# Local attention of a gated block: the next queries are transposed first in a round, the late query embeddings are spread over the seam and rounds 0 to 9, and the first loads come in another order

## The chip, the cores and the metric

The kernel runs on one core of a Trainium2 chip. The metric is the device time of one execution in microseconds (us). The kernel before takes 1314.7 us, the median of three runs between 1314.09 and 1314.88 us. A core has five engines that run side by side, each through its own list of instructions: PE (matrix products; PEld is its loading of weights), DVE (elementwise work), ACT (copies, scaling, exponentials), POOL (more elementwise work) and SP, which here only issues transfers (DMAs).

## The reference, cut to what matters

One decoder block in float32 over 1024 tokens of width 1024. Only the first half concerns the change: a projection, rotary embedding ("rope") of queries and keys, and attention over a window of 128 tokens, cut into blocks of 128 queries that each see their own and the previous block of keys.

```python
def rmsnorm(x, g):
    xf = x.astype(jnp.float32)
    xf = xf * lax.rsqrt(jnp.mean(xf * xf, axis=-1, keepdims=True) + EPS)
    return (xf * g.astype(jnp.float32)).astype(x.dtype)

def apply_rope(x, cos, sin):
    x1, x2 = jnp.split(x.astype(jnp.float32), 2, axis=-1)
    return jnp.concatenate([x1 * cos - x2 * sin, x2 * cos + x1 * sin], axis=-1)

# in reference():
h = rmsnorm(x, mix_norm_g[l])
proj = h @ w_in[l]
qa, ka, va, q_lat, kv_lat, k_r, g_a, g_b = jnp.split(proj, IN_OFFSETS, axis=-1)
qa = apply_rope(qa.reshape(B, S, SWA_HEADS, HEAD_DIM), cos_a, sin_a)   # 8 heads of 64
ka = apply_rope(ka.reshape(B, S, SWA_KV_HEADS, HEAD_DIM), cos_a, sin_a)  # 2 groups
o_a = swa_sink_attention(qa, ka, va, swa_sinks[l])   # window 128, blocks of 128
...
o_b = mla_attention(q_nope, q_rope, k_nope, k_rope, vb)
y = jax.nn.sigmoid(g_a) * (o_a @ w_o_swa[l]) + jax.nn.sigmoid(g_b) * (o_b @ w_o_mla[l])
x = x + y @ w_out[l]
h = rmsnorm(x, ffn_norm_g[l])
x = x + (silu(h @ w_gate[l]) * (h @ w_up[l])) @ w_down[l]
return rmsnorm(x, final_norm_g)
```

## The kernel before

A float32 product is done as three products of rounded halves: both operands are split into a high part (a copy that rounds, on ACT) and a low part (the difference, on DVE), and PE adds high by high, high by low and low by high; lines L305 to L307 are these three. So nearly every operand of PE is made by ACT and then DVE.

The program has these stretches, by the time at which PE works on them:

- 0 to 42 us: the query latents, one tile `ql` for each of eight rows of 128 tokens. The rows come in the order 0, 4, 1, 5, 2, 6, 3, 7. Rows 0 and 4 start from the raw transposed input (`xt`) and the raw weights (`wr`, line L877, four loads), the later ones from the normalised input.
- 38 to 128 us: seven products `st` that stand for the four quarters of the rest of the projection (`product`), each over two halves of the depth and four row blocks `t`. Out of these come queries, keys, values and key latents. Those of blocks 0 to 3 are ready first. Blocks 4 to 7 are "late": their queries are sums of two products, built in the tiles called `w` here and stored to memory (`q_d`, L1287 and L1290).
- 122 to 130 us: the seam, where the last products and the first scores overlap.
- 130 to 300 us: sixteen rounds `it` of local attention (the loop at L1353), one for each pair of head group and block. `ITS` gives their order: group 0 blocks 0 to 3, group 1 blocks 0 to 3, group 0 blocks 4 to 7, group 1 blocks 4 to 7. Each round also holds three products of 12 matmuls (`gate_step`) of the gate projection, whose results are `fa` and `fb`.
- after 300 us: the latent attention, the output projections and the feed-forward part.

In a round the steps for three different blocks are interleaved. For the next block, it+1, `sw_qT` transposes the queries on PE (two matmuls `qT`, L755); ACT copies the high parts (L758, L759), DVE subtracts the low parts (L760, L761) and so makes the tile `qs`; `sw_scores` then does eight matmuls `sc` (L774) with `qs` and the keys `khd`. For the present block, `sw_pT` transposes the probabilities, and for the previous one `sw_pv` multiplies with the values (`o`, L829 and L830). The queries of block it+2 are loaded from `q_d` into `qn` by `sw_q` (L733); those of late blocks are rotated after that by `late_q`, four instructions on DVE (two at L469, one each at L471 and L472).

PE and SP follow the order in which the program is written. In the first 130 us the program itself is ordered by a planner (`beg`, steps are added by `go`): each step has an engine, a cost, what it comes after and sometimes a due time `by`, and the planner lays out all five engines from them. SP's loads have fixed ranks there in the order in which `load_step` is called. In the rounds a scheduler places the instructions of ACT, DVE and POOL.

Of the kernel before, what the change touches and what calls it, by code (L numbers as in the profile page):

```python
# [8 lines left out]
F32 = mybir.dt.float32  # L9
# [8 lines left out]
P = 128  # L18
S = 1024
# [210 lines left out]
def hybrid_block_kernel(  # L230
# [633 lines left out]
    def load_step(*name, kb, emit, use=(), after=()):  # L864
        go("L", *name, eng="S", cost=2000 + kb * 2.6, emit=emit, after=after, use=use, rank=next(turn_of) - 1e6)

    def load_xt(b, k0, k1):
        if b not in xt:
            xt[b] = U("xt", F32, (P, NK, P))
        nc.sync.dma_start(xt[b][:, k0:k1], x_t[b][:, k0:k1])  # L870
# [36 lines left out]
    def ql_load(j):  # L907
        load_step("w", j, kb=416, emit=lambda: load_ql(j), use=(("U", ("wr", j)),))
# [7 lines left out]

    load_step("x", "0a", kb=256, emit=lambda: load_xt(0, 0, 4), use=(("U", ("xt", 0)),))
    ql_load(0)
    load_step("x", 0, kb=256, emit=lambda: load_xt(0, 4, NK), after=[("L", "w", 0)])
    ql_load(1)  # L920
    xt_load(4)
    ql_load(2)
    ql_load(3)
    for i, rows_ in enumerate(((1, 5), (2, 0, 6), (3, 4, 7))):
        for b_ in rows_:
            xs_load(b_)
            if b_ not in RAWS:
                xt_load(b_)
        if i == 1:
            load_step("t", 0, kb=512, emit=lambda: load_tables(0), use=(("U", "t0"),))  # L930
# [49 lines left out]
    for b in ROWS:  # L980
# [7 lines left out]
        go("nm", b, eng="D", cost=1300, emit=lambda b=b: normalize(b), after=[("sp", b), *raw_lo] + [("h0", 1)] * (b == 0), give=("rb", b))  # L988
        for kh in range(2):
            if b in RAWS and b:  # L990
                quad_steps(b, kh, ("rh", "rl"), [("L", "x", b)])
            if (b, kh) != (4, 0):
                quad_steps(b, kh, ("bh", "bl"), [("nm", b)] + [("ql", b)] * (b in RAWS))

# [223 lines left out]
    def kv_steps(b, src, after, by, port):  # L1218
# [2 lines left out]
        go("k3", b, eng="P", cost=600, after=[("km", b)], emit=lambda: rstd_in(rs_k[:, b:b + 1]))  # L1221
        go("k5", b, eng="S", cost=2500, after=[("k4", b)], by=by, emit=lambda: kv_store(b), free=(("kl", b),))

    for t in range(4):
        o = t % 2

# [57 lines left out]
           emit=lambda t=t, c_of=c_of: add(half_of("w2", t), c_of(5), half_of("w2", t), nc.vector))  # L1284
        kv_steps(t + 4, lambda t=t: half_of("w2", t)[:, 256:512], [("C22", t)], 128 + 2 * t, True)
        go("k4", t + 4, eng="D", cost=450, port=True, after=[("k3", t + 4)], emit=lambda t=t: kv_norm(half_of("w2", t)[:, 256:512], t + 4))
        go("qo", t + 4, eng="S", cost=2500, after=[("C22", t)], by=120 + t, emit=lambda t=t: nc.sync.dma_start(q_d[t + 4], half_of("w2", t)[:, 0:256]))  # L1287
        go("C12", t, eng="D", cost=690, after=[("M", 3, 1, t)], by=121 + 1.4 * t, give=("st", 5, t),
           emit=lambda t=t, c_of=c_of: add(half_of("w1", t), c_of(3), half_of("w1", t), nc.vector))
        go("qp", t + 4, eng="S", cost=2500, after=[("C12", t)], by=124 + t, emit=lambda t=t: nc.sync.dma_start(q_d[NB + t + 4], half_of("w1", t)[:, 0:256]))  # L1290
# [50 lines left out]
        k_high(b)  # L1341
        k_low(b)

    def late_q(it):
        b = ITS[it][1]
        qn = sw[it]["qn"]
        rope_nat(halves(qn[:, 0:256], 32), 4, 32, tl_["rope_a"][:, 0, b], tl_["rope_a"][:, 1, b], [halves(qn[:, 0:256], 32)])

    N_SW = 2 * NB
    gates.load_part(1, 0)  # L1350
    V_SUM = {0: (0, 0, 3), 3: (1, 0, 3), 6: (0, 3, 7), 9: (1, 3, 7)}
    V_PART = {2: (0, 0, 3), 5: (1, 0, 3), 8: (0, 3, 7), 12: (1, 3, 7)}
    for it in range(N_SW):  # L1353
        if it + 2 < N_SW:
            sw_q(it + 2)
        if it in V_PART:
            v_parts(*V_PART[it])
        gate_step()
        if it + 1 < N_SW:
            sw_qT(it + 1)  # L1360
        if it in (1, 2, 4, 5):
            late_row({1: 4, 2: 5, 4: 6, 5: 7}[it])
        gate_step()
        if it + 1 < N_SW:
            sw_scores(it + 1)
        if it in (2, 3, 5, 6):
            late_k({2: 4, 3: 5, 5: 6, 6: 7}[it])
        if it + 2 < N_SW and ITS[it + 2][1] > 3:
            late_q(it + 2)
        if it == N_SW - 1:  # L1370
            st.load_to(st.index[("uq", 0)])
            load_lat(4)
        if it >= 1:
            sw_pv(it - 1)
        if it in V_SUM:
            v_sums(*V_SUM[it])
        gate_step()
        sw_pT(it)
        if it + 1 < N_SW:
            sw_exp(it + 1)  # L1380
# [1211 lines left out]
```

## Time and profile before

| | |
|---|---|
| median of 3 runs | 1314.7 us (1314.09 to 1314.88) |
| the profiled execution's own time | 1313.86 us |
| its span, first to last instruction | 1312.1 us |
| PE busy | 1295.6 us, 99% of the span |
| DVE, ACT, POOL busy | 73%, 50%, 43% |
| TensorE's granted clock | 0.999 of full speed on average |

The profiled execution lies 0.84 us below the median. What a stretch costs is read from its own rows, since the share of busy time is a mean over stretches with different limits. In the rows, "idle before" is how long the engine waited, and the arrow names what released it. Matmuls overlap, so their time is read best from the start of one to the start of the next.

### The profile page before, as it was taken

To read this page: it belongs to the slowest core of one execution; us is meant where nothing else is said; L and a number is where in the kernel's file an instruction comes from. 1 tells how busy PE (TensorE), PEld (TensorE's weight loads), DVE (VectorE), ACT (ScalarE), POOL (GpSimd) and SP (SyncE) were. 2 spreads that over 40 slices of the span, in tenths; PEclk is the share of its full clock that TensorE was granted. 3 is DMA by queue.
4 is the path that set the end of the run, shared out by engine and by line. 5 is a ranking of instruction groups with operands and counts; after the bars stand their busy time and mean duration, and the time that the engine had idled before them with its cause. 6 is when DMAs were issued, how large, how long until landed. Compare 5 with 4: busy or idle time off the path is not lost.

```text
span 1312.1 us, 18158 instructions
## 1 busy us (share of the span) xinstructions
PE 1295.6 (99%) x6223; PEld 1082.1 (82%) x6223; DVE 952.2 (73%) x1548; ACT 649.9 (50%) x1299; POOL 561.0 (43%) x518
## 2 busy tenths in 40 slices
PE   9999999999999999999999999999999999999997
PEld 6878787888888888888888888888888888888886
DVE  6998778986778874688889765676666555663964
ACT  7853675675577786644465232232323323634341
POOL 3202557663423365310224468775567621022521
PEclk9999999999999999999999999999999999999999
DMA  9312322436500203895321345743454335995504
GB/s 365 141 47 81 117 101 73 133 105 212 165 17 9 73 34 113 310 267 161 121 89 49 128 154 207 288 171 136 158 184 169 135 126 201 386 383 196 177 16 145
DMA packets 79692, 201.54 MB, mean 154 GB/s; under 512 B 10160, under 2 KB 16816, under 8 KB 78896
## 3 DMA queue, kind: packets, MB, share of 16 engines
q1 hardware_dynamic: 76720, 193.57, 41.3%
q0 software_dynamic: 1440, 4.72, 1.9%
q10 hardware_dynamic: 1440, 2.10, 0.4%
q8 instruction: 49, 0.80, 0.2%
q14 instruction: 43, 0.35, 0.1%
HBM read 138.88 MB, written 57.28 MB: 149 GB/s over the span
## 4 chain that ended last, share of the span: by engine, by line
PE 87%; DVE 4%; ACT 4%; DMA 3%; issue 1%; SPq 0%; POOL 0%; DVEq 0%; ACTq 0%
PE fa L305 8%; PE fa L307 8%; PE fa L306 8%; PE fb L305 6%; PE fb L307 6%; PE fb L306 6%; PE fd L306 5%; PE fd L307 5%; PE fd L305 5%; PE pTb L1763 2%; PE xo L306 2%; PE xo L307 2%; PE xo L305 2%; DMA x<-in_x_dram 1%; PE st L305 1%; PE st L307 1%
## 5 line engine op out<-in xcount | busy, mean ns | idle before, releaser
L299 DVE TENSOR_TENSOR wl<-wr,wl 128x512 fp32r<-128x512 f32 x145 | 148.2, 1044 | 62.1 <-ACT wl L298 61.3
L299 DVE TENSOR_TENSOR lrv<-lr,lrv 128x1024 fp32r<-128x1024 f32 x77 | 105.0, 1396 | 48.4 <-ACT lrv L298 43.0
L298 ACT CAST lrv<-lr 128x1024 fp32r<-128x1024 f32 x77 | 80.1, 1052 | 94.4 <-PE fd L307 58.6
L305 PE MATMUL fd<-lrv 128*128 128x512 f32 x308 | 119.8, 389 | 0.0
L306 PE MATMUL fd<-lrv 128*128 128x512 f32 x308 | 119.8, 389 | 0.0
L307 PE MATMUL fd<-lrv 128*128 128x512 f32 x308 | 119.8, 389 | 0.0
L1747 POOL TENSOR_SCALAR p<-p,denb 128x384 f32<-128x384 f32 (+3 forms) x64 | 48.0, 753 | 89.5 <-DVE denb L1743 75.2
L298 ACT CAST wl<-wr 128x512 fp32r<-128x512 f32 x145 | 83.9, 620 | 1.9 <-PE fa L307 1.6
L299 DVE TENSOR_TENSOR wl<-sm,wl 128x512 fp32r<-128x512 f32 x58 | 52.0, 920 | 30.0 <-ACT wl L298 29.8
L313 POOL TENSOR_TENSOR wr<-wr,sm 128x512 f32<-128x512 f32 x20 | 30.5, 1529 | 95.1 <-DVE wl L299 95.1
L305 PEld LDWEIGHTS fd<-lrv 128*128 128x128 f32 x308 | 57.8, 188 | 12.1
L306 PEld LDWEIGHTS fd<-lrv 128*128 128x128 f32 x308 | 57.8, 188 | 12.0
L307 PEld LDWEIGHTS fd<-lrv 128*128 128x128 f32 x308 | 57.8, 188 | 11.8
L2226 ACT ACTIVATE act<-sm 128x512 f32<-128x512 f32 x11 | 7.0, 632 | 104.1 <-DVE sm L310 104.1
L310 DVE TENSOR_TENSOR ptl<-pTb,pth 128x512 fp32r<-128x512 f32 (+2 forms) x96 | 49.5, 548 | 9.2 <-ACT pth L1774 8.8
L313 POOL TENSOR_TENSOR sm<-wr,wr 128x512 f32<-128x512 f32 (+1 forms) x36 | 41.3, 1153 | 32.1 <-DMA wr<-in_w_gate_dram 28.4
L1733 DVE CUSTOM_DVE_ANT_0 scb<-scb,mask 128x384 f32<-128x384 f32 (+3 forms) x64 | 48.3, 760 | 7.9 <-PE scb L1720 7.4
L1738 ACT ACTIVATE p<-scb,nmb 128x384 f32<-128x384 f32 (+3 forms) x64 | 47.9, 748 | 11.8 <-DVE nmb L1733 8.0
L1774 ACT CAST pth<-pTb 128x512 fp32r<-128x512 f32 (+2 forms) x96 | 43.1, 484 | 10.8 <-PE pTb L1763 10.5
L2226 ACT ACTIVATE act<-pu 128x512 f32<-128x512 f32 x22 | 13.9, 633 | 67.5 <-DVE pu L310 36.7
L305 PE MATMUL fb<-t3h,wl 128*128 128x512 f32 x120 | 47.3, 395 | 0.0
L305 PE MATMUL fb<-t2h,wl 128*128 128x512 f32 x120 | 47.2, 393 | 0.0
(435 smaller groups left out, 4209.6 us busy)
## 6 DMA issues: line engine op xcount, KB each, us to landing
lr<-la_d SPq DMA_DIRECT2D x77, 256.0 KB, 5.4
wr<-in_w_gate_dram SPq DMA_DIRECT2D x22, 512.0 KB, 4.7
wr<-in_w_up_dram SPq DMA_DIRECT2D x22, 512.0 KB, 5.3
la_d<-sd SPq DMA_DIRECT2D x22, 512.0 KB, 4.8
wd<-in_w_down_dram SPq DMA_DIRECT2D x22, 512.0 KB, 7.0
rb_d<-wd SPq DMA_DIRECT2D x22, 512.0 KB, 2.7
lr<-rb_d SPq DMA_DIRECT2D x44, 256.0 KB, 5.4
lr<-in_w_down_dram SPq DMA_DIRECT2D x33, 256.0 KB, 5.4
```

Source lines behind the costliest of these rows:

```text
L298: nc.scalar.copy(hi, src)
L299: (eng or nc.vector).tensor_tensor(lo, src, hi.bitcast(F32), op=ALU.subtract)
L305: nc.tensor.matmul(ps, ah, bh, start=first and i == 0, stop=False, skip_group_check=go_on)
L306: nc.tensor.matmul(ps, ah, bl, start=False, stop=False, skip_group_check=go_on)
L307: nc.tensor.matmul(ps, al, bh, start=False, stop=last and i == n - 1, skip_group_check=go_on)
L310: eng.tensor_tensor(out, a, b, op=ALU.subtract)
L313: eng.tensor_tensor(out, a, b, op=ALU.add)
L1733: nc.vector.tensor_tensor_reduce(s_, s_, m_, 1.0, -NEG, op0=ALU.add, op1=ALU.min, accum_out=nm)
L1738: nc.scalar.activation(p_, s_, AF.Exp, scale=-1.0, bias=t_.pop(("nm", key)), accum_out=den)
L1747: nc.gpsimd.tensor_scalar(p[:, 0:w], p[:, 0:w], den, 0.0, op0=ALU.mult, op1=ALU.add)
L1763: nc.tensor.transpose(pp[:, k], t_["p", key][:, blk(4 * g + k)], ident)
L1774: nc.scalar.copy(hi, pp)
```

## The change

There are three parts.

1. First loads. The second weight tile is loaded before the second half of the first input tile. Input tile 4 (512 KB) is loaded in two halves of 256 KB, after all four weight tiles; its second half is planned behind the first.
2. Order of a round. `sw_qT(it + 1)` comes ahead of the round's first `gate_step`. Two products instead of one stand between the transposes and the scores.
3. Late queries. Group 0's late queries are rotated before they are stored: those of t = 0 and 1 as planned DVE steps in the seam (with stores that wait for them), those of t = 2 and 3 in rounds 0 and 3. Group 1's four late blocks are loaded together (512 KB, in round 5) and rotated in rounds 6 to 9. No round loads or rotates a single late query any more.

```diff
     load_step("x", "0a", kb=256, emit=lambda: load_xt(0, 0, 4), use=(("U", ("xt", 0)),))
     ql_load(0)
+    ql_load(1)
     load_step("x", 0, kb=256, emit=lambda: load_xt(0, 4, NK), after=[("L", "w", 0)])
-    ql_load(1)
-    xt_load(4)
     ql_load(2)
     ql_load(3)
+    load_step("x", "4a", kb=256, emit=lambda: load_xt(4, 0, 4), use=(("U", ("xt", 4)),))
+    load_step("x", 4, kb=256, emit=lambda: load_xt(4, 4, NK), after=[("L", "x", "4a")])
...
-                quad_steps(b, kh, ("rh", "rl"), [("L", "x", b)])
+                quad_steps(b, kh, ("rh", "rl"), [("L", "x", "4a" if kh == 0 else b)])
...
+    def late_q0(t):
+        w = half_of("w2", t)[:, 0:256]
+        rope_nat(halves(w, 32), 4, 32, tl_["rope_a"][:, 0, t + 4], tl_["rope_a"][:, 1, t + 4], [halves(w, 32)])
+
+    def q0_out(t):
+        nc.sync.dma_start(q_d[t + 4], half_of("w2", t)[:, 0:256])
...
-        go("qo", t + 4, eng="S", cost=2500, after=[("C22", t)], by=120 + t, emit=lambda t=t: nc.sync.dma_start(q_d[t + 4], half_of("w2", t)[:, 0:256]))
+        if t < 2:
+            go("rr", t, eng="D", cost=1380, port=True, after=[("C22", t)], by=133 + t, emit=lambda t=t: late_q0(t),
+               use=(("U", ("rr", t)),), free=(("rr", t),))
+            go("qo", t + 4, eng="S", cost=2500, after=[("rr", t)], emit=lambda t=t: q0_out(t))
...
-    def late_q(it):
-        b = ITS[it][1]
-        qn = sw[it]["qn"]
-        rope_nat(halves(qn[:, 0:256], 32), 4, 32, tl_["rope_a"][:, 0, b], tl_["rope_a"][:, 1, b], [halves(qn[:, 0:256], 32)])
+    q1 = []
+
+    def late_q1(t):
+        if not q1:
+            q1.append(U("q1", F32, (P, 4, 256)))
+            nc.sync.dma_start(q1[0], q_d[NB + 4:2 * NB].rearrange("b p c -> p b c"))
+        else:
+            w = q1[0][:, t]
+            rope_nat(halves(w, 32), 4, 32, tl_["rope_a"][:, 0, t + 4], tl_["rope_a"][:, 1, t + 4], [halves(w, 32)])
+            sw[12 + t] = {"qn": w}
...
     for it in range(N_SW):
-        if it + 2 < N_SW:
+        if it + 2 < 12:
             sw_q(it + 2)
         if it in V_PART:
             v_parts(*V_PART[it])
-        gate_step()
         if it + 1 < N_SW:
             sw_qT(it + 1)
+        gate_step()
         if it in (1, 2, 4, 5):
             late_row({1: 4, 2: 5, 4: 6, 5: 7}[it])
+        if it in (0, 3):
+            late_q0({0: 2, 3: 3}[it])
+            q0_out({0: 2, 3: 3}[it])
         gate_step()
         if it + 1 < N_SW:
             sw_scores(it + 1)
         if it in (2, 3, 5, 6):
             late_k({2: 4, 3: 5, 5: 6, 6: 7}[it])
-        if it + 2 < N_SW and ITS[it + 2][1] > 3:
-            late_q(it + 2)
+        if it == 5:
+            late_q1(0)
+        if 6 <= it < 10:
+            late_q1(it - 6)
```

The same numbers of matmuls, copies and rotations are done as before. Since the planner lays out the whole first stretch anew, its instructions also change places among themselves.

On PE, this is where the queries of a round are transposed; it is round 8, whose scores are those of block 9 in the order of `ITS` (`fb` and `fa` are gate products, `pT` the probabilities; a row of dots leaves out the rest of a product). Before, from the end of the round's first product to the scores:

```order
L307 MATMUL fb_2267<-t3h_712,wl_2262 128x512
L755 MATMUL qT_2379<-ident,qn_2229 128x128 x2
L305 MATMUL fa_2399<-t1h_984,wl_2316 128x512
...
L307 MATMUL fa_2399<-t1h_984,wl_2316 128x512
L774 MATMUL sc_2414<-khd_1217,qs_2382 128x256
```

And now, from the transposed probabilities of the round before:

```order
L815 MATMUL pT_2360<-ident,pe_2191 128x128 x4
L755 MATMUL qT_2381<-ident,qn_2252 128x128 x2
L305 MATMUL fb_2290<-t3h_693,wl_2285 128x512
...
L307 MATMUL fb_2290<-t3h_693,wl_2285 128x512
L305 MATMUL fa_2422<-t1h_986,wl_2339 128x512
...
L307 MATMUL fa_2422<-t1h_986,wl_2339 128x512
L774 MATMUL sc_2437<-khd_1219,qs_2384 128x256
```

The two transposes moved past one whole product; the scores stay where they were.

On DVE, this is the end of the seam, from the last of the first block's four maxima to the second block's low parts (`khd` are keys, `pu` a gate result, `lat` key latents, `w` with L469 a late query that is rotated). Before:

```order
L790 TENSOR_TENSOR es_1287<-nm_1285,nsink 128x4
L310 TENSOR_TENSOR khd_1217<-kT_1266,khd_1217 128x128
L310 TENSOR_TENSOR khd_1218<-kT_1266,khd_1218 128x128
L310 TENSOR_TENSOR khd_1217<-kT_1304,khd_1217 128x128
L310 TENSOR_TENSOR khd_1218<-kT_1304,khd_1218 128x128
L313 TENSOR_TENSOR w_117_866<-st_1120,w_117_866 128x512
L299 TENSOR_TENSOR vv_844<-w_117_866,vv_844 128x2x64
L313 TENSOR_TENSOR pu_1337<-fb_1354,pu_1337 128x512
L760 TENSOR_TENSOR qs_1342<-qT_1339,qs_1342 64x2x128
L761 TENSOR_TENSOR qs_1342<-qT_1339,qs_1342 64x2x128
```

And now:

```order
L790 TENSOR_TENSOR es_1308<-nm_1306,nsink 128x4
L310 TENSOR_TENSOR khd_1219<-kT_1286,khd_1219 128x128
L310 TENSOR_TENSOR khd_1220<-kT_1286,khd_1220 128x128
L1214 SCALAR_TENSOR_TENSOR lat_1235<-w_129_964,rs_k,tab_298 128x256
L469 TENSOR_TENSOR rp_1356<-w_129_964,tab_554 128x256
L760 TENSOR_TENSOR qs_1336<-qT_1333,qs_1336 64x2x128
L761 TENSOR_TENSOR qs_1336<-qT_1333,qs_1336 64x2x128
L469 TENSOR_TENSOR rp_1356<-w_129_964,tab_554 128x256
L299 TENSOR_TENSOR wl_1364<-wr_975,wl_1364 128x512
L471 TENSOR_TENSOR w_129_964<-rp_1356 128x4x32
L472 TENSOR_TENSOR w_129_964<-rp_1356 128x4x32
L313 TENSOR_TENSOR pu_1354<-fb_1369,pu_1354 128x512
```

The gate result and a pair of keys no longer stand ahead of the low parts; one key latent and half of a rotation do.

On SP, these are the first loads (`xt` 163 is input tile 0; `xt` 174 before and 192 now is tile 4). What was and what now stands, as a difference:

```order
 L877 DMA wr_167<-in_w_ql_dram 128x832
-L870 DMA xt_174<-in_x_t_dram 128x1024
+L877 DMA wr_174<-in_w_ql_dram 128x832
 L870 DMA xt_163<-in_x_t_dram 128x512
 L877 DMA wr_183<-in_w_ql_dram 128x832
-L877 DMA wr_192<-in_w_ql_dram 128x832
-L434 DMA x_198<-in_x_dram 128x1024
-L870 DMA xt_210<-in_x_t_dram 128x1024
+L870 DMA xt_192<-in_x_t_dram 128x512
+L434 DMA x_199<-in_x_dram 128x1024
+L870 DMA xt_205<-in_x_t_dram 128x1024
+L870 DMA xt_192<-in_x_t_dram 128x512
```

Input tile 4 moved from the fourth place to the seventh and the tenth; from the load behind that on the two lists agree.

## Rows read from the trace of the kernel before

**Rows 1.** The page: busy time, share of the span and instructions of each engine.

```profile
PE 1295.6 (99%) x6223; PEld 1082.1 (82%) x6223; DVE 952.2 (73%) x1548; ACT 649.9 (50%) x1299; POOL 561.0 (43%) x518
```

**Rows 2.** Waits of PE, 130 to 306 us: us in total, times, longest.

```profile
PE sc L774 <- DVE qs L760: 2.1, 3, 1.3
PE sc L774 <- DVE qs L761: 0.8, 5, 0.2
```

**Rows 3.** Timeline of PE, block 1: start, us, instruction, [idle before <-releaser].

```profile
131.18 0.38 PE L755 MATMUL qT<-ident,qn 128*128 128x128 f32 x2
...
133.95 0.39 PE L307 MATMUL fb<-t2h,wl 128*128 128x512 f32 x1
135.62 0.39 PE L774 MATMUL sc<-khd,qs 128*128 128x256 f32 x1 [1.29 <-DVE qs L760]
136.17 1.07 PE L774 MATMUL sc<-khd,qs 128*128 128x256 f32 x7 [0.16 <-DVE qs L761]
137.08 0.40 PE L305 MATMUL fa<-hh,wl 128*128 128x512 f32 x1
```

**Rows 4.** Timeline of PE, block 2.

```profile
143.05 0.38 PE L755 MATMUL qT<-ident,qn 128*128 128x128 f32 x2
...
145.79 0.39 PE L307 MATMUL fa<-t1h,wl 128*128 128x512 f32 x1
...
146.97 0.40 PE L829 MATMUL o<-pth,vv 128*128 128x512 f32 x1
```

**Rows 5.** Timeline of PE, blocks 6, 9 and 12, ahead of and behind the scores.

```profile
189.13 0.39 PE L307 MATMUL fa<-hh,wl 128*128 128x512 f32 x1
...
191.15 0.39 PE L496 MATMUL kT<-ident,kd 128*128 128x128 f32 x2
...
222.93 0.39 PE L307 MATMUL fa<-t1h,wl 128*128 128x512 f32 x1
...
225.37 0.40 PE L829 MATMUL o<-pth,vv 128*128 128x512 f32 x1
...
257.21 0.39 PE L307 MATMUL fa<-hh,wl 128*128 128x512 f32 x1
...
258.88 0.40 PE L829 MATMUL o<-pth,vv 128*128 128x512 f32 x1
```

**Rows 6.** Windows of two rounds: us, then PE, PEld, DVE, ACT, POOL busy, clock, DMA.

```profile
202.80:214.00 11.20, 11.04 (x54) 8.85 (x54) 10.89 (x23) 7.51 (x22) 8.97 (x11) 1.00 0.49 154
248.20:259.60 11.40, 11.23 (x56) 9.07 (x55) 11.11 (x22) 5.05 (x16) 8.26 (x11) 1.00 0.26 78
```

**Rows 7.** Groups by line and shape, 130 to 305 us: busy us, mean ns | idle before.

```profile
L469 DVE TENSOR_TENSOR rp<-qn,tab 128x256 f32<-128x256 f32 x16 | 11.3, 733 | 0.0
L760 DVE TENSOR_TENSOR qs<-qT,qs 64x256 fp32r<-64x256 f32 x15 | 6.3, 418 | 2.3 <-ACT qs L759 1.8
```

**Rows 8.** Timeline of DVE ahead of the seam, a rotation of one block's queries.

```profile
99.62 0.75 DVE L469 TENSOR_TENSOR rp<-st,tab 128x256 f32<-128x256 f32 x2
100.41 0.29 DVE L471 TENSOR_TENSOR qn<-rp 128x128 f32<-128x128 f32 x1
```

**Rows 9.** Windows of the seam.

```profile
120.00:124.00 4.00, 4.00 (x22) 3.32 (x21) 2.29 (x9) 1.65 (x7) 1.62 (x3) 1.00 0.18 66
128.46:133.00 4.54, 4.54 (x22) 3.74 (x21) 2.30 (x11) 2.94 (x15) 2.32 (x4) 1.00 0.03 10
```

**Rows 10.** Timeline of PE, the stalls of the first stretch.

```profile
10.43 0.94 PE L1001 MATMUL ql<-wr,h 128*128 128x416 f32 x2 [1.58 <-DMA wr<-in_w_ql_dram]
...
12.98 0.67 PE L305 MATMUL ql<-wv,hh 128*128 128x416 f32 x1
...
69.99 0.47 PE L305 MATMUL st<-wl,hh 128*128 128x512 f32 x1 [0.77 <-ACT wl L858]
```

**Rows 11.** Windows of the first stretch.

```profile
10.00:20.00 10.00, 9.52 (x44) 7.76 (x45) 6.54 (x14) 6.73 (x12) 3.11 (x5) 1.00 1.03 414
40.00:50.00 10.00, 10.00 (x50) 9.03 (x49) 10.00 (x16) 9.96 (x18) 1.03 (x2) 1.00 0.43 153
```

## Prediction

> **What bounds the kernel now.** I read the page first, then PE's waits, then PE's timeline wherever it waits, then the other engines in those places. PE is busy for 1295.6 of 1312.1 us [rows 1], so a change of order can gain only what PE loses in single places, and those can be counted. In the local attention PE waits almost only for one thing, the low parts of the transposed queries that DVE makes (`qs`): 2.1 and 0.8 us [rows 2]. A wait understates the loss, because a matmul is pipelined behind the one before it. I therefore measure from the start of the last product's last matmul to the start of whatever follows the eight scores. Where nothing is late that is 146.97 - 145.79 = 1.18 us [rows 4]. In block 1 it is 137.08 - 133.95 = 3.13, an excess of 1.95 [rows 3]. In blocks 6, 9 and 12 it is 2.02, 2.44 and 1.67, excesses of 0.84, 1.26 and 0.49 [rows 5]; blocks 8 and 11 are like 12, at about 0.5 each. All other blocks are near 1.18.
>
> So there are about 1.95 us to be had in the seam and 0.84 + 1.26 + 3 x 0.5 = 3.6 us in the rounds. In the first 120 us two waits of PE matter here, 1.58 us for a weight tile at 10.43 and 0.77 us at 69.99 [rows 10].
>
> **Rounds, the transposes moved up.** Nothing is added, two matmuls change place. In block 2 the transposes start at 143.05 and the last matmul of the one product in between at 145.79 [rows 4], so the scores can start 2.97 us after the transposes. Twelve matmuls at 0.228 us are 2.73 us, so with a second product in between the scores come 5.70 us after. The longest that the scores ever took before they could run freely is block 1: 136.17 - 131.18 = 4.99 us [rows 3]. With 5.70 us of cover all five stalls should be gone. I leave 0.2 us for raggedness: gain 3.4. The bounds are 0 (the copies on ACT and DVE stay where they were, since a scheduler places them) and 3.6.
>
> **Rounds, the rotations.** Before, eight rotations lie in rounds 6 to 13. Now four lie in rounds 6 to 9, one each in rounds 0 and 3, two in the seam. A rotation is two L469, one L471, one L472: alone 0.75 + 2 x 0.29 = 1.3 us [rows 8]. In the rounds the same L469 takes 733 ns instead of 375 [rows 7, 8], so a rotation there may cost up to twice as much, 2.6. Rounds 10 to 13 lose one each: DVE in round 11 goes from 11.11 of 11.40 us to some 8.5 to 9.8 [rows 6]. This does not move PE by itself, but it takes DVE away from being the bound in those rounds. Rounds 6 to 9 keep theirs; the window of round 7 has DVE at 10.89 of 11.20 us [rows 6], which is what could keep the stalls of blocks 8 and 9 alive (first rival). Rounds 0 and 3 have idle DVE, and the stores that now follow these rotations stand on SP ahead of a gate load, for whose data PE never waits in the rounds [rows 2]. I cost both at nothing; without that cover it would be 1.3 to 2.6 us each.
>
> The doubled L469 fits the Trainium skill, "GPSIMD Engine Reference", section 1 (Specifications): POOL's way to the on-chip memory is shared with DVE, with contention for instructions that have two inputs there, as L469 has. By that rule the two rotations in the seam would cost 2.6 us while POOL is idle and 5.2 while it is busy; the row that speaks is POOL's share there, 1.62 of 4.00 and 2.32 of 4.54 us [rows 9], so neither alone.
>
> **Seam.** The second block's scores get the same 5.70 us of cover, but DVE's list ahead of them changes: a gate result and a pair of keys go behind, one key latent (about 0.5 us) and half of the rotation of t = 2 (0.38 to 0.73 us) come in front. From 4.99 that gives at most 4.99 + 0.5 + 0.73 = 6.2 us against 5.70, so 0.5 us late at worst; with the ragged start that a late pair has (136.17 - 135.62 = 0.55 instead of about 0.15, [rows 3]) I leave 0.6 us of the 1.95. Gain 1.35, bounds 0 and 1.95.
>
> Two whole rotations, 2.6 us alone and 5.2 contended, come in front of the first block's scores. DVE is idle there for 4.00 - 2.29 = 1.71 us between 120 and 124, and 4.54 - 2.30 = 2.24 behind them [rows 9]. At 2.6 that leaves under 1 us to push the first block's `qs`, its maxima or the first gate product. As there is some idle time ahead of 120 too, I take 0.2 us of loss, with bounds 0 and 5.2 - 1.71 = 3.5.
>
> **First loads.** PE's stall at 10.43 ends with a weight tile [rows 10]. If that is the third, 256 + 2 x 416 + 512 + 256 + 416 = 2272 KB were issued up to it; now it is 256 + 3 x 416 = 1504 KB, 768 KB less. At 414 GB/s [rows 11] this is 1.9 us, so the 1.58 us could go wholly. The fourth tile gains 512 KB or 1.27 us. But input tile 4 is now complete only after 3712 KB, 1440 KB behind what PE waited for at 10.43: 10.43 + 3.56 = 14.0 us, and then ACT and DVE must split it. Row 4 starts at 12.98 [rows 10] and would start at about 11.8; its first half takes 2.4 us, so its second half is wanted at 14.2 and ready at about 15. What is won on row 0 is mostly waited for again in row 4. Behind it PE depends on what DVE prepares, which has the same work: DVE is busy for all of the 10 us from 40 to 50 [rows 11], and the stall at 69.99 would grow by what PE comes earlier. I take 0, bounds -0.8 (row 4 late, passed on) and +1.1.
>
> The Trainium skill, "DMA: Bandwidth & Descriptors", section "Anatomy of one DMA", gives each transfer a fixed part of about 2 us beside its bytes, which speaks against loading tile 4 in two. Paid in full it would make this term -2, by estimate. Between 10 and 20 us the trace shows transfers that overlap without a gap (share 1.03, [rows 11]), so the fixed part should be hidden.
>
> The rest of the planner's new order in the first 130 us holds the same instructions. PE's order by kind is nearly the same there, and I have no row for a gain or a loss: 0, bounds -1 and +0.8 (the stall at 69.99 [rows 10] gone).
>
> **Sum.** 3.4 + 1.35 - 0.2 + 0 + 0 = 4.55 us. The profiled execution took 1313.86 us, so 1309.3; the median of the runs lies 0.84 above it, and from it the forecast is 1314.7 - 4.55 = 1310.15, rounded 1310.2. Behind round 15 the instructions stand in the same order, so what is won there is kept to the end.
>
> **Rivals.**
>
> A. DVE, not the order on PE, is the bound in rounds 6 to 9. For it: 10.89 of 11.20 us [rows 6], and the rotations there stay. Against: round 11 has a DVE as busy as that and loses only 0.5 us in its scores, so a full DVE is not yet a late `qs`. Then only blocks 11, 12 and the seam gain, 2 x 0.5 + 1.35 - 0.2 = 2.15: 1312.6.
>
> B. The start costs. Row 4 waits for its second half and passes it on: 4.55 - 0.8 = 3.75, 1311.0. For it: 14.0 us against 14.2 leaves no time for the split. Against: DVE, not PE, sets the pace behind it [rows 11]. With the fixed part that the Trainium skill, "DMA: Bandwidth & Descriptors", section "Anatomy of one DMA", states for the added transfer, it would be 1312.2; this changes no chance here.
>
> C. Slower: the weights' low parts come late. ACT's and DVE's four instructions for `qs` now come a whole product earlier, ahead of the halves of the gate weights `wl` that this next product needs. DVE's part is 2 x 0.42 = 0.84 us [rows 7]. If PE then waits for `wl` in ten of the fifteen rounds, that is 8.4 us, less the 4.55: 3.9 slower, 1318.6. It decides from six rounds on. For it: in rounds like 7 and 11 DVE has under 0.4 us left [rows 6]. Against: PE's list of waits has none for `wl` in all rounds [rows 2].
>
> D. The seam eats it. The rotations are contended and lie in front of the first scores: -3.5 there, nothing of the 1.35, +3.4 in the rounds: 1314.8.
>
> E. All stalls go and the start gains too: 3.6 + 1.95 + 1.1 = 6.65: 1308.0.
>
> **How the numbers follow.** Forecast 0.45, A 0.17, B 0.12, C 0.07, D 0.09, E 0.10. A difference of 0.2%, 2.6 us, is about what a measurement of this kernel tells from none; the line is 1312.1. The forecast's own range is 1309 to 1311.5, and B and E lie on its side; of A a fifth does. Faster: 0.45 + 0.12 + 0.10 + 0.03 = 0.70. Within: the rest of A and most of D, 0.14 + 0.08 = 0.22. Slower: C and a little of D, 0.08. The range from 1307.8 to 1313.6 leaves out C, most of D and little at the lower end.
>
> **What would show it.** Right: PE's waits between 130 and 300 us hold almost nothing for `qs`, the distance around the scores is 1.18 us in blocks 6, 8, 9, 11 and 12, and block 1 is down from 3.13 to some 1.8; the sixteen rounds are 3 to 5 us shorter. A would show as waits for `qs` in blocks 8 and 9, C as waits of PE for `wl` in the rounds, D as a wait at block 0 near 126 us, B as the 69.99 row coming later. The forecast is wrong if the first score of round 0 comes more than 1 us later than before, or if a stretch behind 300 us changes its length.

## The result

The change makes the kernel slower: 1323.9 us, the median of 6 runs (1321.4 to 1328.1), against 1314.4 for the kernel before in the same comparison. The ratio is 1.0073, with a 95% interval of 1.0055 to 1.0090, so 7 to 12 us were lost where 4.5 were forecast to be won. The profiled execution took 1324.0 us, its span is 1322.3.

The first rows are the page of the kernel after, its lines of busy time and of TensorE's granted clock in 40 slices.

```profile
PE 1296.8 (98%) x6223; PEld 1083.3 (82%) x6223; DVE 957.5 (72%) x1548; ACT 650.5 (49%) x1299; POOL 558.9 (42%) x518
...
PEclk9999999999999999999999999999999999999999
```

PE does the same work as in [rows 1]. The 10.2 us of longer span are time in which it waits, plus some time at half clock that the 40 slices are too coarse to show. The next rows are PE's waits in the kernel after, from 130 to 306 us (us in total, times, longest).

```profile
PE sc L774 <- DVE qs L760: 6.3, 3, 3.7
PE fb L305 <- DVE pu L313: 2.0, 1, 2.0
PE fb L305 <- DVE sm L313: 1.5, 2, 1.3
PE sc L774 <- DVE qs L761: 0.7, 4, 0.2
PE fa L305 <- DVE go L313: 0.6, 1, 0.6
```

The wait that the change was to remove has grown from 2.1 to 6.3 us [rows 2], and there is a new kind: gate products (`fa`, `fb`) that wait until DVE has taken the last result out of their bank. From 300 us on both kernels run alike, as forecast: the lag is 10.8 us at the last scores and 10.6 at the last matmul.

Where the lag arises is read from the first instruction behind each block's scores, after minus before. Block 0 stands at +2.6 us. Of this 1.4 is there by 70 us, and most of the rest is no loss: six matmuls of the last product and two key transposes, which the planner moved ahead of these scores. Block 1 is at +3.4, block 2 at +4.9, block 4 at +7.3, block 5 at +9.7, block 10 at +9.8 and block 11 at +11.4; from block 12 on it stays at +10.8. So, beside the 1.4 us of the first stretch, it is lost in four places: ahead of block 1, behind block 1, in blocks 4 and 5, and behind block 10.

**Ahead of block 1, the seam.** The timeline of PE in the kernel after, answering to [rows 3]:

```profile
129.42 0.41 PE L755 MATMUL qT<-ident,qn 128*128 128x128 f32 x2
...
134.91 0.39 PE L307 MATMUL fb<-t2h,wl 128*128 128x512 f32 x1
139.03 0.39 PE L774 MATMUL sc<-khd,qs 128*128 128x256 f32 x1 [3.72 <-DVE qs L760]
139.58 1.07 PE L774 MATMUL sc<-khd,qs 128*128 128x256 f32 x7 [0.16 <-DVE qs L761]
140.49 0.50 PE L305 MATMUL fa<-hh,wl 128*128 128x512 f32 x1
```

The cover was there: the second product's last matmul starts 5.5 us after the transposes. But the scores could run freely only 10 us after them, and the excess rose from 1.95 to 140.49 - 134.91 - 1.18 = 4.40 us. DVE's timeline in the same place says why.

```profile
136.59 1.20 DVE L1214 SCALAR_TENSOR_TENSOR lat<-w,rs_k,tab 128x256 f32<-128x256 f32 x1 [2.19 <-POOL rs_k L516]
137.72 0.81 DVE L469 TENSOR_TENSOR rp<-w,tab 128x256 f32<-128x256 f32 x1
138.55 0.42 DVE L760 TENSOR_TENSOR qs<-qT,qs 64x256 fp32r<-64x256 f32 x1
```

DVE stood 2.19 us ahead of the last key latent, for a factor from POOL, with the low parts queued behind it. POOL's timeline:

```profile
135.01 1.04 POOL L806 TENSOR_TENSOR pe<-pe,den 128x512 f32<-128x512 f32 x1
136.01 0.54 POOL L516 TENSOR_TENSOR rs_k<-rs_k,neg_half 128x1 f32<-128x1 f32 x1
```

POOL computed that factor (L516) only after the division of the first block's softmax (L805, L806). In the kernel before, the last of these factors ended at 123.4 us, well ahead of that softmax.

**Behind block 1, the clock.** The windows of the kernel after: us, then PE, PEld, DVE, ACT and POOL busy, granted clock, DMA.

```profile
135.00:139.00 4.00, 0.30 (x2) 0.00 (x0) 2.35 (x3) 0.63 (x2) 3.15 (x4) 1.00 0.08 28
...
140.00:142.00 2.00, 2.00 (x10) 1.67 (x9) 1.97 (x6) 0.00 (x0) 0.00 (x0) 0.66 0.80 302
142.00:144.00 2.00, 2.00 (x6) 1.54 (x5) 0.94 (x3) 1.93 (x5) 0.00 (x0) 0.50 0.44 83
```

After four microseconds in which PE was busy for 0.30, the granted clock goes to 0.50, that is 1.2 instead of 2.4 GHz, until 144 us. Matmuls then follow each other every 0.43 us instead of 0.23, and the lag grows by 1.5 us with no wait on PE at all. The Trainium skill, "TensorE: Matmul & The Clock Gate", Part 1 ("The HAM clock gate"), states that an idle PE falls to 1.2 GHz and that activity gives the clock back; the trace agrees (0.50 behind the stop, 0.99 from 144 to 146 us).

**In the rounds, ACT and a rotation.** Two groups of the kernel after between 130 and 315 us (busy us, mean ns | idle before them and what ended it):

```profile
L708 ACT ACTIVATE wr<-wr,gT 128x256 f32<-128x256 f32 x56 | 24.4, 499 | 14.6 <-DMA wr<-in_w_gt_dram 14.6
...
L760 DVE TENSOR_TENSOR qs<-qT,qs 64x256 fp32r<-64x256 f32 x15 | 6.3, 418 | 12.0 <-ACT qs L759 11.9
```

DVE waited 12.0 us for ACT's copies of the queries, where it was 2.3 of which 1.8 for ACT [rows 7]. ACT waited 14.6 us for gate weights from memory, against 4.6 before. In block 4, where PE waited 1.44 us for `qs`, ACT had stood 2.56 us for such weights, and the four exponentials came next, ahead of the copies.

The two longest waits of the new kind have other causes. In block 5 DVE was busy without a pause with the rotation of t = 3, which part 3 put into round 3, and took the gate result out of its bank behind it; the timelines of DVE, and in the last row of PE:

```profile
176.35 1.98 DVE L469 TENSOR_TENSOR rp<-w,tab 128x256 f32<-128x256 f32 x2
...
181.00 0.69 DVE L313 TENSOR_TENSOR sm<-fb,pu 128x512 f32<-128x512 f32 x1
181.84 0.47 PE L305 MATMUL fb<-t4h,wl 128*128 128x512 f32 x1 [1.25 <-DVE sm L313]
```

The rotation's four instructions take from 176.35 to 179.83, 3.5 us. Ahead of block 11 (1.97 us at 255.14) ACT had waited 4.70 us for gate weights, and DVE 0.93 us for a copy of ACT that stood behind them.

### The profile page after: what moved, and what is told of

It is laid out like the page before. It is cut to its first block, busy times and chain, and to the rows that moved or that the text cites. A ratio compares the mean times of both kernels' runs of the same rounds, so it can differ in the third digit from the quotient of the medians.

```text
span 1322.3 us, 18170 instructions
## 1 busy us (share of the span) xinstructions
PE 1296.8 (98%) x6223; PEld 1083.3 (82%) x6223; DVE 957.5 (72%) x1548; ACT 650.5 (49%) x1299; POOL 558.9 (42%) x518
## 4 chain that ended last, share of the span: by engine, by line
PE 78%; DVE 1%; ACT 1%; DMA 1%; issue 1%; POOL 0%; SPq 0%; ACTq 0%; DVEq 0%
PE fa L306 7%; PE fa L305 7%; PE fa L307 7%; PE fb L305 5%; PE fb L306 5%; PE fb L307 5%; PE fd L307 5%; PE fd L305 5%; PE fd L306 5%; PE pTb L1785 2%; PE xo L305 2%; PE xo L306 2%; PE xo L307 2%; PE ob L1823 1%; PE scb L1740 1%; PE ob L1822 1%
## 5 line engine op out<-in xcount | busy, mean ns | idle before, releaser
L299 DVE TENSOR_TENSOR wl<-wr,wl 128x512 fp32r<-128x512 f32 x145 | 152.9, 1077 | 56.2 <-ACT wl L298 55.7
```

What stands on the lines that cost most here:

```text
L299: (eng or nc.vector).tensor_tensor(lo, src, hi.bitcast(F32), op=ALU.subtract)
```

## The experiments

Each is timed against the kernel before on the same chip. The parts are: 1 the first loads, 2 the transposes ahead of the first product, 3 the late queries. "Alone" means in the kernel before.

| kernel | median us | ratio to before (95%) | lag at block 1, 5, 15 |
|---|---|---|---|
| the change | 1323.9 | 1.0073 (1.0055 to 1.0090) | +3.4, +9.7, +10.8 |
| part 1 alone | 1313.8 | 0.9998 (0.9988 to 1.0007) | -0.6, -0.8, -0.8 |
| part 2 alone | 1319.6 | 1.0039 (1.0024 to 1.0054) | -1.2, +2.2, +5.7 |
| part 3 alone | 1318.9 | 1.0035 (1.0022 to 1.0048) | +3.0, +5.5, +4.8 |
| parts 2 and 3 | 1322.1 | 1.0065 (1.0048 to 1.0082) | +2.6, +7.2, +7.3 |

The lag is that of one profiled execution each. Five kernels below do the same work in the same order as the kernel before up to 120 us, and stand 0.2 to 0.9 us behind it at block 0; so a lag of less than 1 us tells little, and the median decides.

**Part 1 alone** (`e1_loads`). 

> Part 1 of the change alone (first loads). Theory S (each part loses in its own place: the loads in the first 42 us, the late queries in the seam and behind it, the turned transposes not at all): 1.4 us slower than before, all of it by 70 us, in waits of PE for the diagonal tiles of POOL. Rival T (the turned transposes are what costs, because ACT now has the exponentials ahead of the copies of the queries): the loads alone stay within 1 us of before.

It makes no difference that can be measured, so theory S falls for the loads. PE does wait 1.8 us for POOL's diagonal tiles there, as expected, but it no longer waits for the weight tiles, and at block 0 it is 0.55 us early.

**Part 2 alone** (`e2_turn`). 

> Part 2 alone (transposes ahead of the round's first product). Theory S: 2 to 4 us faster than before, the waits for qs in the rounds gone. Rival T: 4 us or more slower, with PE waiting for qs behind ACT's exponentials and for banks that DVE frees late.

Rival T holds in the time: 5.1 us slower by the ratio. The seam won more than was forecast, the excess of block 1 went to 0.09 us. The rounds lost it and more. Of PE's waits there only 1.8 us are for `qs` and 1.4 for banks; the largest, 3.1 us, are transposes that wait (2.2 of these at block 8, shown below).

**Part 3 alone** (`e3_late`). 

> Part 3 alone (late queries rotated in the seam and rounds 0, 3, 6 to 9). Theory S: 5 to 8 us slower, the second scores more than 2 us later and ACT waiting for late gate weights. Rival T: within 2 us of before, since the transposes stand where they did.

Slower by 4.6 us, between the two theories and nearer to S, with an excess of 5.3 at block 1 and 9.2 us in which ACT waited for gate weights. So this part has a loss of its own.

**Parts 2 and 3** (`e4_turn_late`). 

> Parts 2 and 3 without the first loads. Theory S: 8 us slower than before, that is the whole change less the 1.4 us of the loads. Rival T: the same, so this run tells only whether the loads' part adds up or also disturbs the seam; if the planner's other order from the loads makes the seam bad, it would be within 3 us of before.

8.5 us by the ratio. The two parts' losses nearly add up, and the loads are not what spoils the seam.

**The place of the copies on ACT** (`e7_turn_ahead`). Part 2 alone, with one thing changed (the transposes of round 0 stay where part 2 has them):

```diff
+        if it + 2 < N_SW:
+            sw_qT(it + 2)
         if it + 1 < N_SW:
             sw_exp(it + 1)
```

The transposes of the next round are written right ahead of the exponentials, at the end of the round, and no longer at the next round's start. PE has nothing in between, so its order is that of part 2 alone. 

> Part 2 alone, but the copies of a round's queries are emitted ahead of the exponentials instead of behind them; on PE the order is the same as with part 2 alone (1319.6 us). Theory T (what costs in the turned rounds is that ACT does the four exponentials, and whatever these wait for, ahead of the copies): the copies start 0.5 to 1.2 us after the transposes instead of 2.0 to 6, the waits for qs go, and the time is 1314 to 1317, with the rest of the loss in transposes that now wait for the rotations. Rival V (the loss is the late rotations, and the weights and banks that DVE frees late): 1319 or more, as with part 2 alone.

1312.2 us, ratio 0.9986 (0.9977 to 0.9995): 7.0 us below part 2 alone by the ratios, and faster than the kernel before. PE's order is the same. On ACT 28 of the 31 instructions that changed places between 130 and 296 us are these copies; on DVE the scheduler moved 34 of 297, which no run takes apart from it. ACT's timeline in the kernel before, where the transposes of block 5 started at 175.63, behind the exponentials:

```profile
174.63 0.38 ACT L802 ACTIVATE pe<-sc,nm 128x128 f32<-128x128 f32 x1
...
176.05 0.37 ACT L758 CAST qs<-qT 64x256 fp32r<-64x256 f32 x1 [0.44 <-PE qT L755]
```

In part 2 alone, where they started at 175.14, ahead of them:

```profile
175.62 0.59 ACT L298 CAST pth<-pT 128x512 fp32r<-128x512 f32 x1
176.21 0.37 ACT L802 ACTIVATE pe<-sc,nm 128x128 f32<-128x128 f32 x1
...
177.25 0.37 ACT L802 ACTIVATE pe<-sc,nm 128x128 f32<-128x128 f32 x1
...
177.60 0.36 ACT L758 CAST qs<-qT 64x256 fp32r<-64x256 f32 x1
```

And in this kernel, where they started at 170.70:

```profile
170.96 0.59 ACT L298 CAST pth<-pT 128x512 fp32r<-128x512 f32 x1 [0.90 <-PE pT L815]
171.44 0.36 ACT L758 CAST qs<-qT 64x256 fp32r<-64x256 f32 x1
171.83 0.37 ACT L759 CAST qs<-qT 64x256 fp32r<-64x256 f32 x1
172.22 0.37 ACT L802 ACTIVATE pe<-sc,nm 128x128 f32<-128x128 f32 x1
```

The copies start 0.74 us after the transposes instead of 2.46. In a quiet round this costs nothing, since the cover is 5.7 us. But the exponentials themselves wait for the maxima and stand behind the scaling of gate weights, and whatever holds them now holds the next queries too: in part 2 alone the copies came 5.98 and 5.40 us after the transposes in blocks 3 and 4. DVE's wait at the low parts for these copies shows it (part 2 alone, then this kernel, 130 to 315 us):

```profile
L760 DVE TENSOR_TENSOR qs<-qT,qs 64x256 fp32r<-64x256 f32 x15 | 6.3, 418 | 10.4 <-ACT qs L759 10.1
L760 DVE TENSOR_TENSOR qs<-qT,qs 64x256 fp32r<-64x256 f32 x15 | 6.3, 418 | 1.0 <-ACT qs L759 0.7
```

What is left of PE's waits here is this one row, for late queries whose rotation is not done (the transposes come a product earlier than before):

```profile
PE qT L755 <- DVE qn L472: 2.2, 3, 1.3
```

In part 2 alone the worst of these stands at block 8. The profile names no releaser there, but DVE's last instruction of the rotation ends 0.1 us ahead of the transposes. PE's timeline, with that row of DVE between:

```profile
206.94 0.60 PE L815 MATMUL pT<-ident,pe 128*128 128x128 f32 x4
209.39 0.28 DVE L472 TENSOR_TENSOR qn<-rp 128x128 f32<-128x128 f32 x1
209.77 0.42 PE L755 MATMUL qT<-ident,qn 128*128 128x128 f32 x2 [2.23 <-issue]
```

A window behind it (columns as above):

```profile
212.00:214.00 2.00, 2.00 (x7) 1.54 (x6) 1.78 (x5) 1.10 (x3) 1.81 (x3) 0.50 0.92 324
```

A stop of 2.2 us, and again half clock behind it: the lag rises by 3.4 us in this one round. With the copies ahead, the transposes of this block wait 0.59 us.

**Only the seam turned, with the loads** (`e8_seam_turn`). The transposes come ahead of the first product in round 0 alone.

```diff
+        if it == 0:
+            sw_qT(it + 1)
         gate_step()
-        if it + 1 < N_SW:
+        if it + 1 < N_SW and it != 0:
             sw_qT(it + 1)
```

> Part 1, and part 2 in round 0 only; late queries as before. With part 2 alone the excess of block 1 went from 1.95 to 0.09 us, and the loads alone were 0.5 us earlier at the seam. Theory T: 1.5 to 2.7 us faster than before, about 1312. Rival U (what a place wins in the first rounds is given back by the next wait, as the rounds are bound by ACT and DVE): within 0.7 us of before.

1313.8 us, ratio 1.0004 (0.9995 to 1.0012). Rival U holds in the time. In the profiled execution, which at 1316.1 us was the longest of eleven, block 1 is 1.84 us early, but block 2, with one product of cover again, then waits; PE's timeline, and behind it a window:

```profile
143.95 0.39 PE L307 MATMUL fa<-t1h,wl 128*128 128x512 f32 x1
146.41 0.39 PE L774 MATMUL sc<-khd,qs 128*128 128x256 f32 x1 [2.08 <-DVE qs L760]
```

And the window:

```profile
148.00:150.00 2.00, 2.00 (x6) 1.60 (x6) 1.98 (x3) 1.84 (x4) 1.88 (x3) 0.50 0.21 83
```

**No rotation in the seam** (`e9_late_rounds`). Part 3 alone, the four rotations of group 0 in rounds 0 to 3; the sum that they work on gets a due time of its own (117.4 + t us in the plan), since its store now gives it none.

```diff
-        if t < 2:
-            go("rr", t, ...)
-            go("qo", t + 4, ...)
...
-        if it in (0, 3):
-            late_q0({0: 2, 3: 3}[it])
-            q0_out({0: 2, 3: 3}[it])
+        if it < 4:
+            late_q0(it)
+            q0_out(it)
```

> Part 3 alone, but all four rotations of group 0 lie in rounds 0 to 3 and none in the seam, so the planner's order of the first stretch is that of before. Theory S2 (part 3 loses in the seam because the rotations there push the last key latent's chain behind the first softmax on POOL, which holds the second queries on DVE and the gate loads on SP): no wait above 2 us at block 1, at most 2 us slower than before, where part 3 alone was 4.7 slower. Rival R (the stores ahead of the gate loads on SP and the longer held buffers are what costs): 4 us slower or more, with ACT waiting for gate weights in rounds 1 to 4.

1316.9 us, ratio 1.0021 (1.0012 to 1.0031), 2.8 us slower and between the two theories. Block 1 is as in the kernel before (excess 1.75), so the seam's loss is gone. Blocks 3 and 4 have excesses of 1.10 and 1.85 instead of 0.33 and none. ACT waited 5.6 us for gate weights, about as before, so the stores on SP are not the cause; more rotations on DVE in rounds 1 to 3 fit, but no run takes them apart there.

**The last key latent first** (`e10_latent_first`). The two rotations in the seam come after it in the plan, and have no due time any more.

```diff
-go("rr", t, eng="D", cost=1380, port=True, after=[("C22", t)], by=133 + t, ...
+go("rr", t, eng="D", cost=1380, port=True, after=[("C22", t), ("k4", 7)], ...
```

> Part 3 alone with one edge more: the two rotations in the seam come after the last key latent's normalisation in the planner's order. The same rotations, stores and loads as in part 3 alone. Theory S2: the excess at block 1 falls from 5.3 us to 2 or 3, and the whole to 1 to 3 us slower than before. Rival R: still 4 us or more slower.

1320.0 us, ratio 1.0041 (1.0026 to 1.0057), which is rival R's time. The excess of block 1 fell only from 5.3 to 3.4 us, and the whole did not fall: now the rotations themselves stand ahead of the low parts. DVE's timeline in this kernel:

```profile
133.41 0.75 DVE L469 TENSOR_TENSOR rp<-w,tab 128x256 f32<-128x256 f32 x2
134.08 0.28 DVE L299 TENSOR_TENSOR vv<-w,vv 128x128 fp32r<-128x128 f32 x1
134.28 1.13 DVE L471 TENSOR_TENSOR w<-rp 128x128 f32<-128x128 f32 x1
135.33 1.08 DVE L472 TENSOR_TENSOR w<-rp 128x128 f32<-128x128 f32 x1
136.33 1.14 DVE L469 TENSOR_TENSOR rp<-w,tab 128x256 f32<-128x256 f32 x2
137.50 0.42 DVE L760 TENSOR_TENSOR qs<-qT,qs 64x256 fp32r<-64x256 f32 x1
```

**The whole change with the copies ahead** (`e11_all_ahead`). The edit is that of the run above, in the changed kernel. 

> The whole change, with the copies of a round's queries emitted ahead of the exponentials. Theory T (the turned rounds lose only through the exponentials ahead of the copies; part 2 alone went from 1319.6 to 1312.2 by this): 5 to 8 us less than the change, 1316 to 1319, and what is left is the seam. Rival W (in the whole change the copies are late because ACT waits for gate weights that SP loads late, so their place does not matter): within 2 us of the change, 1322 to 1325.

1318.2 us, ratio 1.0031 (1.0017 to 1.0044): 5.5 us below the change by the ratios, so rival W falls. The excess of block 1 stays at 4.8.

**Loads and the copies ahead** (`e12_loads_ahead`). The same edit with part 1. 

> Part 1, and part 2 with the copies ahead of the exponentials; late queries as before. If the two gains add (part 1 alone -0.3 of median and -0.8 us in the rounds, part 2 so -1.7 of median): 1311 to 1312, 2 to 3 us faster than before. Rival: the loads' part adds nothing, since part 2's remaining waits are for rotations: 1312.2.

1312.7 us, ratio 0.9987 (0.9978 to 0.9996): the loads add nothing.

**Rotations a round earlier** (`e13_ahead_early`). With the copies ahead:

```diff
-            sw_q(it + 2)
+            sw_q(it + 3)
...
-            late_q(it + 2)
+            late_q(it + 3)
```

> Part 2 with the copies ahead of the exponentials, and each single late query loaded and rotated one round earlier than before (rounds 5 to 12). Theory T: the transposes no longer wait for a rotation (0.63, 0.33 and 1.37 us went there), so 1 to 2.3 us less than without, about 1310.5. Rival X (the rotations now meet the late keys in rounds 5 and 6 and one more buffer is held, so the loads of gate weights come later): 1312 or more.

1315.0 us, ratio 1.0006 (0.9997 to 1.0015). Rival X holds in the time. The waits for rotations went and others came; the largest in this kernel's list of PE's waits:

```profile
PE fb L305 <- DVE pu L313: 3.0, 2, 2.8
```

Between 241 and 249 us, around that wait of 2.8 us, the granted clock stayed at 1.00, so such a stop is not followed by half clock every time.

**The first softmax later** (`e14_first_softmax_late`). Part 3 alone, `sw_exp(0)` written behind the planned stretch; POOL's factor for the last key latent so comes ahead of the first division.

```diff
-emit=lambda: (sw_scores(0), sw_exp(0)), ...
+emit=lambda: sw_scores(0), ...
...
+    sw_exp(0)
     for it in range(N_SW):
```

> Part 3 alone, with the first block's exponentials emitted behind the planned stretch; so POOL does the last key latent's factor ahead of the first softmax's division, not behind it, and ACT the last keys ahead of the exponentials. Rotations, stores and loads are those of part 3 alone. Theory S2 (the last key latent behind POOL's division is what holds the second queries and SP): the excess at block 1 falls from 5.3 to at most 3 us, the first gate load is issued 2 us earlier, and the time is 1314.5 to 1316.5. Rival Z (the three rotations on DVE hold the second queries, wherever the latent stands): excess still above 4, time 1318 or more.

At block 1 theory S2 is right: the excess fell from 5.27 to 1.05 us, and the first gate load was issued at 133.8 instead of 136.6. But the time is 1317.4 us (ratio 1.0024, 1.0015 to 1.0034), over the range of S2. The runs spread from 1314.8 to 1319.9, and in the longest, the profiled one, blocks 2 to 4, with one product of cover, have excesses of 1.1 to 2.1.

**No rotations of group 0 at all** (`e15_no_rotation`). Part 3 alone, with the body of `late_q0` empty, so that these queries stay unrotated.

```diff
     def late_q0(t):
-        w = half_of("w2", t)[:, 0:256]
-        rope_nat(halves(w, 32), 4, 32, ...)
+        pass
```

> Part 3 alone with the four rotations of group 0's late queries left out (these queries stay unrotated; planner's order, stores, loads and buffers are those of part 3 alone). Theory D (part 3 loses by the rotations' time on DVE in the seam and rounds 0 and 3, and what queues behind them): 1 us of before or less, 1313 to 1315.5. Theory S2 (by the place of the last key latent, which stays as in part 3 alone): 1317 to 1319, block 1 with an excess of 4 us or more.

1318.8 us, ratio 1.0040 (1.0026 to 1.0054), and an excess of 5.2 at block 1. DVE's row for the last key latent:

```profile
134.95 1.21 DVE L1213 SCALAR_TENSOR_TENSOR lat<-w,rs_k,tab 128x256 f32<-128x256 f32 x1 [2.19 <-POOL rs_k L516]
```

The same 2.19 us of waiting without the rotations' work, so D falls: what part 3 loses ahead of block 1 is the new place of that latent's factor. Once that is mended, the rotations' own time shows (the run with the latent first). Behind block 1 the rotation in round 3 does count: at block 4 the lag grows by 1.0 us in part 3 alone and by 0.1 here.

**Rotations ahead of the scores** (`e16_rotation_first`). The run with the copies ahead, the late query's rotation written ahead of the second product.

```diff
+        if it + 2 < N_SW and ITS[it + 2][1] > 3:
+            late_q(it + 2)
         gate_step()
         if it + 1 < N_SW:
             sw_scores(it + 1)
-        if it + 2 < N_SW and ITS[it + 2][1] > 3:
-            late_q(it + 2)
```

> Part 2 with the copies ahead of the exponentials, and the rotation of a late query emitted ahead of the round's second product and scores instead of behind them. Theory T: the three waits of transposes for a rotation (2.3 us) shrink to under 0.5 us and the time is 1310 to 1311. Rival X (DVE is full in these rounds, so the maxima come later and the exponentials with them): 1312 or more.

1312.7 us, ratio 0.9990 (0.9981 to 0.9999), like the run it is built on and in rival X's range. The waits for rotations are gone (2.2 us), as theory T had it, and others of 1.3 us in all took their place.

**Both mended in the whole change** (`e17_both_mended`). The copies ahead of the exponentials in every round, and the first block's exponentials behind the transposes of block 1:

```diff
         if it == 0:
             sw_qT(1)
+            sw_exp(0)
         gate_step()
```

The rest is as in the two runs that it joins: the planned step keeps `sw_scores(0)` alone, and the transposes of later rounds are written ahead of the exponentials.

> The whole change with the copies ahead of the exponentials in all rounds, and the first block's exponentials behind the planned stretch, so that the last key latent's factor stands ahead of the first softmax on POOL. If the two causes found are all, what is left is near before: 1313 to 1315.5. Rival D (the rotations on DVE early on are a cause of their own): 1316 or more, with the loss in rounds 1 to 5.

1311.0 us (10 runs, 1310.1 to 1312.3), ratio 0.9977 (0.9968 to 0.9986). All three parts of the change are in it, and it is 3.0 us faster than the kernel before by the ratio, better than expected and the lowest of the kernels tried. PE's timeline at block 1, answering to [rows 3]:

```profile
134.46 0.39 PE L307 MATMUL fb<-t2h,wl 128*128 128x512 f32 x1
134.68 1.12 PE L774 MATMUL sc<-khd,qs 128*128 128x256 f32 x8
135.64 0.40 PE L305 MATMUL fa<-hh,wl 128*128 128x512 f32 x1
```

1.18 us, nothing lost. And all that PE waits for between 130 and 306 us:

```profile
PE fb L305 <- DVE pu L313: 1.2, 1, 1.2
PE sc L774 <- ACT pe L802: 0.5, 1, 0.5
PE fa L305 <- DVE go L313: 0.2, 1, 0.2
```

## Why the prediction was wrong

**What held.** The excesses could be won: with both orders mended 0.8 us at block 9 is all that is left of some 5.5, though 1.4 us of waits for banks took a part back. The second product does give 5.7 us of cover: in that kernel the scores start 5.7 us after the transposes in eleven of fifteen rounds, and block 1 loses nothing. The loads were costed at nothing and measured as nothing, though not by the mechanism given. In part 1 alone row 0 ended 1.7 us earlier and new waits for POOL's diagonal tiles, 1.8 us, gave it back; in the change PE waited 1.5 us for weight tiles even so, and row 0 ended as before. The fixed part of a transfer, which the prediction priced at up to 2 us, did not show in part 1 alone. What is won or lost in the rounds is kept to the end within 0.6 us in thirteen of the sixteen changed kernels; the profiled executions of the other three lose 0.8 to 1.9 us behind them.

**The step that failed, in the rounds.** "With 5.70 us of cover all five stalls should be gone". The 4.99 us that it was held against were measured from transposes that came behind the exponentials in time. On ACT the copies follow the four exponentials in both kernels: from block 2 on they start 0.85 to 1.73 us after the last of them before, 0.34 to 0.59 now. So the prediction's own case for a gain of 0, that the copies "stay where they were", is nearly what came true: cover and latency grew together. But 0 was not the lower end. DVE stood waiting for the copies, the transposes now ask for the late rotations a product sooner, and stops brought half clock. Priced by the runs, the place of the copies, with what the scheduler makes of it on DVE, is 7.0 us in part 2 alone and 5.5 in the whole change. The order of PE was compared, the order of ACT at the same place was not. Rival C looked at the right kind of thing from the wrong side: in the change PE's list has no wait for `wl`.

**The step that failed, in the seam.** "One key latent (about 0.5 us)" was priced by the duration of an instruction that had moved in front of the low parts. It cost 2.19 us of waiting for POOL, whose factor had moved behind a softmax, and then took 1.20. The row stood in the order shown; what it waits for was not followed to POOL. The excess became 4.40 us where 0.6 was forecast. Rival D named the seam with a price of 3.5, but for the rotations' time, and the run without rotations shows that this was not what held block 1 in part 3.

**Terms at nothing.** The rotation in round 3 was costed at nothing because DVE had idle time there. In the change it took 3.5 us of DVE, more than the 2.6 named without that cover, and PE waited 1.25 us behind it; in part 3 alone block 4 loses 1.0 us with it and 0.1 without. The granted clock was 1.00 in every row read, and the text let it stay there. Stops of PE of some 1.2 to 3.9 us were followed by half clock in nine of the profiled executions, and in the change this is 1.5 of the 10.2 us.

**The prediction's own sign.** It called itself wrong if the first score of round 0 came more than 1 us later. It came 3.0 us later, but little of this is loss: 1.4 us in the first stretch, the rest mostly work that the planner moved ahead.

**Left open.** The lag at blocks 4 and 5 and behind block 10 (2.4, 2.4 and 1.7 us) is mostly gone in the runs with the copies ahead and with both causes mended. The rows above name what stood in the way in each, but how it divides between ACT's exponentials, its wait of 14.6 us for gate weights and the rotation was not measured. Nor is it settled why the gate weights came later, or why blocks 2 to 4 lose with the first softmax later and part 2 left out.

## What to carry to other kernels

A step that is moved earlier on one engine must be looked up in the lists of all engines that finish it: cover on PE is worth only what its followers do not spend on something else first, and a few lines written in another order on ACT were 7 us here. Price an instruction that moves ahead of a critical one by what it waits for, on whichever engine that is, and not by how long it runs. Where a change gains on PE and loses as a whole, undo its parts one by one and then mend orders rather than undo: the change with two orders mended gained 3.0 of the 4.55 us forecast.

## What the runs showed of the hardware

After a single stop of 2.1 to 3.7 us, PE's granted clock was 0.5 for 2 us or more in the change, in part 2 alone (212 to 214 us) and in the run with only the seam turned (148 to 150 us); a stop of 2.8 us with the rotations a round earlier was not followed by it, while one of 1.2 us with the latent first was (0.50 from 174 to 176 us). So the length of a stop alone does not tell, and a stall can cost a good part of itself once more behind it (1.2 us behind the 2.23 of part 2 alone), in rows that show no wait. And a rotation's last two instructions took 1.13 and 1.08 us in the seam (the run with the latent first), while POOL was at work, against 0.29 alone [rows 8].
